# RMSNorm factors from one constant product over split sums of squares, in a two-layer decoder trunk

## The chip, the cores and the metric

The kernel runs on one core of one Trainium2 chip. The metric is the device time of one execution in microseconds, and lower is better. TensorE (PE) multiplies matrices, ScalarE (ACT) evaluates functions and copies, VectorE (DVE) does elementwise work, GpSimd (POOL) does little here, and SyncE (SP) issues nearly all DMAs. Each engine runs its own queue in order and waits on semaphores of the others. PE writes its results to PSUM, eight banks of 128 x 512 fp32; operands lie in SBUF, which has 128 partitions.

## The reference

The input is one sequence of 1024 tokens with 1024 channels. There are two layers. The first mixes tokens with a gated linear recurrence, the second with stick-breaking attention of 16 heads. Each is followed by a SwiGLU feed-forward network (FFN) of width 2816. An RMSNorm stands ahead of each of these four sub-layers and one more at the end.

```python
def rms_norm(x, g):
    xf = x.astype(jnp.float32)
    y = xf * lax.rsqrt(jnp.mean(xf * xf, axis=-1, keepdims=True) + RMS_EPS)
    return (y * g.astype(jnp.float32)).astype(x.dtype)

def reference(...):
    h = x
    for layer in range(2):
        hn = rms_norm(h, mix_norm[layer])
        mixed = rg_lru_block(hn, ...) if layer == 0 else stick_breaking_attention(hn, ...)
        h = h + mixed
        h = h + swiglu_ffn(rms_norm(h, ffn_norm[layer]), ffn_w_in[layer], ffn_w_out[layer])
    return rms_norm(h, final_norm)
```

All inputs and the output are fp32.

## The kernel before

**Layout.** Activations lie transposed: channels are on partitions, in 8 blocks of 128, and tokens run along the free axis, in two halves of 512 (`n` = 0, 1). One tile of 128 x 512 is one block of one half.

**Precision.** Every operand of a large product is split into a high and a low part of a shorter format (fp32r): a copy on ACT gives the high part, a subtraction on DVE gives the low part. A product is then three matmuls of 128x512, high x high, high x low and low x high (`mm3`, L598 to L600). The FFN also uses a scheme of seven products in place of eight (products 0, 1, 2, 3, 4, 6, 5 in this order, each of four `mm3`), so that combinations of weights and of activations are formed on DVE.

**The norm.** The gain is folded into the activations ahead of the product, and the factor 1/sqrt(mean + eps), one number for each token, is multiplied onto the product's result. So it is needed late, but it is needed on all 128 partitions. For each half the kernel gathers the squares of the 8 blocks in one 128 x 512 tile (`sacc`, `acc` or `rbc`) with ACT and DVE. What is left is a sum over the partitions, a root, and a copy to all partitions. That is done in four steps:

1. Sums: four fp32 matmuls with a 128x128 slice of the tile as the left operand and a column of ones as the right one. The sums come out as columns of 4 values, tokens on partitions (`column_stats`, `stats_mm`, `column_sums`).
2. Root: a small Sqrt on ACT and five or six small DVE instructions on 128x4 or 128x8, with one Newton step, to `rcol`.
3. Spread: four fp32 matmuls of 128x128 for each half. A column of `rcol`, read 128 times, is multiplied by the identity, which puts the factors along the free axis on all partitions (`spread`, L645; `factors`, L1381).
4. In the recurrence and in attention DVE copies the result to SBUF (`rbc`, L787 and L2178). The FFN reads it in PSUM (`ob`).

An fp32 matmul of this kind leaves two records in the profile, so four of them stand as x8.

**Order.** It is written out by hand for each engine. The four places are:

- *Recurrence.* PE multiplies the first four column groups for tokens of half 0, block by block as data arrive. Then it runs the four groups of half 1 (`second(0)` to `second(3)`, 24 matmuls each). Both halves' sums and spreads share the one bank that belongs to the fourth group. Behind this a planner (`lru_plan`) orders the rest from estimated costs.
- *FFN of each layer.* The first step (`f` = 0) is special; the norm stands in the loop's first pass (`s_ == 0`, `f` = 1): the sums behind the fourth product (`k == 3`) and the spreads behind the sixth (`k == 5`). DVE and ACT meanwhile split weights for this step and the next (`nw` is the next one: `a_lo` L1114, `s12`, `s2`, `s3` L1097 to L1103, `do_s4` L1106, `b_lo` L1123, `c_lo` L1133 and L1134), copy products out of PSUM (`post`, L1283 to L1296), and apply the gate (L1301 to L1307): the product of G and the factor, Silu, the factor again for the up branch, the product of the two. `b_lo` of a step stands behind the gate's first instruction of that step, and PE needs its result in the third matmul of the third product.
- *Attention.* `attention_plan` lists every task of the stage with an engine, an estimated cost and a rank. `Plan.emit` simulates the engines with these costs and emits the tasks in that order. A root of another table costs 1.3 there, and a handoff between engines 0.15. Queries and keys, multiplied by the factor, are split and moved by DMAs on SP's queue, and the first score product (`z`, L2035) needs them.

The final norm has a path of its own (`end_plan`, `finish`) and is not touched by the change.

## Time and profile before

| What | Value |
| --- | --- |
| time, median of 3 runs | 2174.35 us (2174.34 to 2174.76) |
| time of the profiled execution | 2175.16 us |
| span in the profile | 2173.0 us |
| PE busy | 2160.0 us, 99% of the span |
| DVE busy | 1709.4 us, 79% |
| ACT busy | 1086.4 us, 50% |
| granted PE clock | 1.0 over the whole span |

A row of the timeline has the start in us, the duration, the engine, the line of the kernel, the operation, output<-inputs by the program's names, shapes, and how many records are merged in it. In square brackets stands how long the engine idled ahead of it and who ended that wait. PEld rows are weight loads, which run beside PE's matmuls. The start of a matmul is recorded and its end is modelled: rows of PE overlap, so a cost on PE is read from one start to the next. The chain that ended last is followed back from the last instruction to whatever released each step.

### The profile page before, as it was taken

What the parts mean: (1) busy time and instruction counts of PE and PEld (TensorE: products, weight loads), DVE (VectorE), ACT (ScalarE), POOL (GpSimd) and SP (SyncE); (2) the same over time, 40 slices, a digit from 0 to 9 for tenths busy, and PEclk for the clock granted to TensorE, in tenths of its full rate; (3) what the DMA queues carried; (4) which work ended last, traced back from release to release, by engine and by line L of the source; (5) the groups of instructions that cost most, each with busy time, mean ns of one, the idle gap of its engine ahead of it and who ended that gap; (6) DMA issues with size and microseconds to landing.
All of it is one profiled execution on the core that took longest, in us unless ns stands there. A gap on an engine that the chain in (4) does not pass through costs nothing.

```text
span 2173.0 us, 27239 instructions
## 1 busy us (share of the span) xinstructions
PE 2160.0 (99%) x10066; PEld 1793.4 (83%) x10066; DVE 1709.4 (79%) x2429; ACT 1086.4 (50%) x1775; POOL 29.1 (1%) x38
## 2 busy tenths in 40 slices
PE   9999999999999999999999999999999999999998
PEld 7888888888888888888888888888888888888787
DVE  7988678667777887878888888877877777787887
ACT  5577445344444544555555555544534444454555
POOL 0000020000000000000000000002000000000000
PEclk9999999999999999999999999999999999999999
DMA  4111312344444753443333333542133444467442
GB/s 176 40 49 49 118 47 70 105 141 141 141 159 132 271 204 122 146 143 100 90 105 88 104 90 102 156 166 81 59 116 117 146 143 147 142 235 242 127 162 85
DMA packets 133317, 274.62 MB, mean 126 GB/s; under 512 B 15296, under 2 KB 23872, under 8 KB 133184
## 3 DMA queue, kind: packets, MB, share of 16 engines
q1 hardware_dynamic: 132768, 272.36, 38.5%
q8 instruction: 79, 1.29, 0.2%
q10 hardware_dynamic: 416, 0.52, 0.1%
q14 instruction: 54, 0.44, 0.1%
HBM read 176.88 MB, written 70.78 MB: 114 GB/s over the span
## 4 chain that ended last, share of the span: by engine, by line
PE 96%; DVE 2%; ACT 1%; issue 0%; DMA 0%; SPq 0%; POOL 0%; DVEq 0%; ACTq 0%; POOLq 0%
PE p_ps L600 18%; PE p_ps L598 18%; PE p_ps L599 18%; PE qk_ps L598 4%; PE qk_ps L600 4%; PE qk_ps L599 4%; PE z_ps L2035 3%; PE av_ps L2083 3%; PE wt_ps L2066 3%; PE a_ps L599 3%; PE a_ps L598 3%; PE a_ps L600 3%; PE ob_ps L599 2%; PE ob_ps L598 2%; PE ob_ps L600 2%; PE g_ps L599 1%
## 5 line engine op out<-in xcount | busy, mean ns | idle before, releaser
L598 PE MATMUL p_ps<-vh,wbh 128*128 128x512 f32 x524 | 204.4, 390 | 1.2 <-ACT ta L1741 1.2
L600 PE MATMUL p_ps<-vh,wal 128*128 128x512 f32 x524 | 204.4, 390 | 0.5 <-DVE wal L1114 0.4
L598 PE MATMUL p_ps<-vh,wch 128*128 128x512 f32 x524 | 204.5, 390 | 0.2 <-ACT held L1519 0.2
L600 PE MATMUL p_ps<-vh,wbl 128*128 128x512 f32 x524 | 204.5, 390 | 0.0
L600 PE MATMUL p_ps<-vh,wcl 128*128 128x512 f32 x524 | 204.3, 390 | 0.0
L599 PE MATMUL p_ps<-vl,wbh 128*128 128x512 f32 x524 | 204.1, 389 | 0.0
L598 PE MATMUL p_ps<-vh,wah 128*128 128x512 f32 x524 | 204.1, 389 | 0.0
L599 PE MATMUL p_ps<-vl,wch 128*128 128x512 f32 x524 | 204.1, 389 | 0.0
L599 PE MATMUL p_ps<-vl,wah 128*128 128x512 f32 x524 | 204.1, 389 | 0.0
L1119 ACT CAST wbh<-sb 128x1024 fp32r<-128x1024 f32 (+2 forms) x69 | 69.6, 1009 | 198.1 <-DVE sb L1103 198.1
L2047 ACT ACTIVATE F<-z_ps 128x512 f32<-128x512 f32 (+3 forms) x188 | 92.1, 490 | 99.3 <-PE z_ps L2035 97.9
L2071 ACT CAST th<-wt_ps 128x512 fp32r<-128x512 f32 x192 | 92.2, 481 | 84.3 <-PE wt_ps L2066 77.1
L2054 DVE TENSOR_TENSOR_SCAN F<-F,unit 128x128 f32<-128x128 f32 (+3 forms) x128 | 104.9, 821 | 33.4 <-ACT F L2047 32.4
L2075 DVE TENSOR_TENSOR tl<-wt_ps,th 128x512 fp32r<-128x512 f32 x192 | 104.7, 546 | 16.6 <-ACT th L2071 16.4
L600 PEld LDWEIGHTS p_ps<-vh,wal 128*128 128x128 f32 x524 | 98.4, 188 | 22.1 <-DVE wal L1114 1.8
L598 PEld LDWEIGHTS p_ps<-vh,wbh 128*128 128x128 f32 x524 | 98.4, 188 | 21.8 <-ACT ta L1741 1.6
L600 PEld LDWEIGHTS p_ps<-vh,wbl 128*128 128x128 f32 x524 | 98.4, 188 | 21.5 <-DVE wbl L1123 1.1
L598 PEld LDWEIGHTS p_ps<-vh,wch 128*128 128x128 f32 x524 | 98.4, 188 | 21.0 <-ACT held L1519 0.7
L600 PEld LDWEIGHTS p_ps<-vh,wcl 128*128 128x128 f32 x524 | 98.4, 188 | 20.8 <-DVE wcl L1133 0.3
L599 PEld LDWEIGHTS p_ps<-vl,wah 128*128 128x128 f32 x524 | 98.4, 188 | 20.5
L599 PEld LDWEIGHTS p_ps<-vl,wbh 128*128 128x128 f32 x524 | 98.4, 188 | 20.4
L599 PEld LDWEIGHTS p_ps<-vl,wch 128*128 128x128 f32 x524 | 98.4, 188 | 20.5
(430 smaller groups left out, 5499.1 us busy)
## 6 DMA issues: line engine op xcount, KB each, us to landing
raw<-in_ffn_w_in SPq DMA_DIRECT2D x88, 512.0 KB, 3.7
vl<-pd SPq DMA_DIRECT2D x128, 256.0 KB, 3.6
pd<-U SPq DMA_DIRECT2D x90, 256.0 KB, 2.3
raw<-in_ffn_w_out SPq DMA_DIRECT2D x28, 512.0 KB, 4.1
raw<-in_attn_w_qkv SPq DMA_DIRECT2D x24, 512.0 KB, 3.8
kh<-qh SPq DMA_DIRECT2D x64, 128.0 KB, 2.3
kl<-ql SPq DMA_DIRECT2D x64, 128.0 KB, 2.3
acc<-pd SPq DMA_DIRECT2D x28, 256.0 KB, 2.6
```

The costliest lines, as they stand in the source:

```text
L598: nc.tensor.matmul(ps, lhsT=wh, rhs=mh, start=first, stop=False, **kw)
L599: nc.tensor.matmul(ps, lhsT=wh, rhs=ml, start=False, stop=False, **kw)
L600: nc.tensor.matmul(ps, lhsT=wl, rhs=mh, start=False, stop=last, **kw)
L1119: nc.scalar.copy(self.full(self.wb), self.full(self.sb))
L2035: nc.tensor.matmul(ps[:, 0:n], lhsT=lhsT, rhs=rhs, start=i == 0, stop=i == 1)
L2047: nc.scalar.activation(F, Z.pop(c)[:, 0:n], AF.Sigmoid, scale=-SC)
L2054: V.tensor_tensor_scan(rev, rev, unit[:, NB - n :][:, ::-1], 0.0, op0=ALU.mult, op1=ALU.add)
L2066: nc.tensor.transpose(tp[:, c : c + P], F[:, (kb % 4) * P : (kb % 4 + 1) * P], ident)
L2071: nc.scalar.copy(WH[u][:, c:], TP[u][:, c:])
L2075: V.tensor_sub(WL[u][:, c:], TP.pop(u)[:, c:], f32(WH[u])[:, c:])
L2083: nc.tensor.matmul(ps[:, c:], lhsT=VV[q][:, kb, hx], rhs=t.pop(u)[:, c:], start=kb == 4 * G and i == 0, stop=kb == 3 and i == 1,)
```

## The change

At the four places the sums, the small root chain, the spread and the copy are replaced by a class `Factors`. For each half it does this:

- `hi`, `lo`: splits the tile of square sums into a high and a low part, one ACT copy and one DVE subtraction of 128x512;
- `sums`: two matmuls of 128x512. The left operand is one constant column (-2^-41, tile `minus`) read 128 times, so that every partition gets the sum for every token, in place;
- `root`: Abs_reciprocal_sqrt on ACT, 128x512 from PSUM, with scale and a bias operand that undo the constant;
- `square`: the square of that on ACT;
- `newton` and `out`: two DVE instructions of 128x512 which make one Newton step. In the FFN, `out` writes to PSUM, where the gate reads it.

In the recurrence both halves' sums stand between `second(0)` and `second(1)`, in the banks of the third and fourth column group. In the FFN, `hi` and `lo` stand at `k == 2`, the sums at `k == 4`, and the remaining four steps at `k == 4` too, behind `a_lo`, `s2` and `s3` of the next weights. They borrow one FFN tile and the two small tiles `ta` and `tb`. In attention the planner gets seven tasks for each half in place of five, with new costs. At the start there are two one-column memsets and one one-column copy more.

```diff
     for n in range(NH):
-        t = plan.add("pe", 0.95, fn["sums", n], [known["acc", n]], -17 + 2 * n)
-        t = plan.add("act", 0.25, fn["root", n], [t], -17 + 2 * n, "sqrt")
-        t = plan.add("dve", 1.0, fn["factor", n], [t], -17 + 2 * n)
-        t = plan.add("pe", 1.05, fn["spread", n], [t], -16 + 2 * n)
-        factors.append(plan.add("dve", 0.62, fn["rbc", n], [t], -16 + 2 * n))
+        t = plan.add("act", 0.5, fn["s_hi", n], [known["acc", n]], -17 + 2 * n)
+        t = plan.add("dve", 0.6, fn["s_lo", n], [t], -17 + 2 * n)
+        t = plan.add("pe", 0.46, fn["sums", n], [t], -17 + 2 * n)
+        t = plan.add("act", 0.62, fn["root", n], [t], -17 + 2 * n, "root")
+        t = plan.add("act", 0.5, fn["square", n], [t], -17 + 2 * n)
+        t = plan.add("dve", 0.66, fn["newton", n], [t], -17 + 2 * n)
+        factors.append(plan.add("dve", 0.66, fn["rbc", n], [t], -17 + 2 * n))
...
+    minus = cp.tile([P, 128], F32R, name="minus")
+    fresh = tiny[:, 60:61]
+    nc.gpsimd.memset(fresh, -(2.0**-41))
+    nc.vector.tensor_copy(minus[:, 0:1], fresh)
+    nc.gpsimd.memset(tiny[:, 61:62], EPS * 2.0**-20)
+
+    class Factors:
+        def __init__(self, src, hi, lo, ps, w, ww, out):
+            self.src, self.parts, self.ps, self.w, self.ww, self.to = src, (hi, lo), ps, w, ww, out
+        def hi(self):
+            nc.scalar.copy(self.parts[0], self.src)
+        def lo(self):
+            nc.vector.tensor_sub(self.parts[1], self.src, f32(self.parts[0]))
+        def sums(self):
+            for i, t in enumerate(self.parts):
+                nc.tensor.matmul(self.ps, lhsT=minus[:, 0:1].broadcast_to([P, P]), rhs=t, start=i == 0, stop=i == 1)
+        def root(self):
+            nc.scalar.activation(self.w, self.ps, AF.Abs_reciprocal_sqrt, bias=tiny[:, 61:62], scale=-(2.0**11))
+        def square(self):
+            nc.scalar.square(self.ww, self.w)
+        def newton(self):
+            nc.vector.scalar_tensor_tensor(self.ww, self.ps, -EPS * 2.0**-31, self.ww, op0=ALU.add, op1=ALU.mult)
+        def out(self):
+            nc.vector.scalar_tensor_tensor(self.to, self.ww, 1.5 * 2.0**-10, self.w, op0=ALU.add, op1=ALU.mult)
+        def rest(self):
+            self.root()
+            self.square()
+            self.newton()
+            self.out()
...
-        column_stats(sacc[0], bank, 0)
+        again = lambda k, dt=F32: sp.tile([P, NB], dt, tag=f"fr{k}", name="again")
+        sums = [
+            Factors(sacc[n], again(n, F32R), again(2 + n, F32R), pa[FIRST[3 - n]][1], rbc[n], again(4 + n), rbc[n])
+            for n in range(NH)
+        ]
+        sums[0].hi()
+        sums[0].lo()
         second(0, range(ND))
-        spread_to(0)
+        sums[1].hi()
+        sums[1].lo()
+        for t in sums:
+            t.sums()
+        for t in sums:
+            t.rest()
...
-        column_stats(sacc[1], bank, 1)
         second(1, range(ND))
-        spread_to(1)
         second(2, range(ND))
...
-            UT = [gp.tile([P, S], F32, name=f"U{i}") for i in range(3)]
+            GT, UT = [big("G", i) for i in range(2)], [big("U", i) for i in range(2)]
...
+            t = big("U", 2, F32R)
+            parts = (half(t, 0), half(t, 1)), [pair_tile(x, F32R) for x in ("ta", "tb")]
+            sums = [Factors(acc[n], *parts[n], half(ob, n), acc[n], rbc[n], half(ob, n)) for n in range(NH)]
...
-                        elif k == 3:
-                            stats_mm()
-                        elif k == 5:
-                            factors()
+                        elif k == 4:
+                            for t in sums:
+                                t.sums()
+                            UT.append(big("U", 2))
+                            ta, tb = (pair_tile(x) for x in ("ta", "tb"))
...
                         w.d_lo()
                         if nw:
                             nw.a_hi()
+                        if s_ == 0:
+                            for t in sums:
+                                t.hi()
+                                t.lo()
                     elif nw:
...
                             nw.a_lo()
                             nw.s2()
                             nw.s3()
+                            if s_ == 0:
+                                for t in sums:
+                                    t.rest()
...
+        def sums_hi(n):
+            SUM[n] = Factors(
+                rbc[n], own([P, NB], f"oo{n}", F32R, "oo"), own([P, NB], f"F{8 + n}", F32R),
+                bank(psO, "o", n, "st_ps"), own([P, NB], f"F{10 + n}"), own([P, NB], f"tl{n}"), rbc[n],
+            )
+            SUM[n].hi()
```

More of the change, by code (lines that the diff above doesn't have):

```diff
@@ L573, in trunk @@
     rcol = cp.tile([P, NT], F32, name="rcol")
-    cp.tile([P, 120], F32, name="edge_l")
+    minus = cp.tile([P, 128], F32R, name="minus")
[26 more added lines that the diff above has]
+            self.out()
     def load_raw(src):
@@ L628, in proc @@
             self.w[self.order[i]] = (k3(hi), k3(lo))
-    def rstd(dst, ms):
-        n = dst.shape[-1]
-        sq = cp.tile([P, max(n, 4)], F32, tag="rs_s", name="rs_s", bufs=2)[:, 0:n]
-        t = cp.tile([P, max(n, 4)], F32, tag="rs_t", name="rs_t", bufs=2)[:, 0:n]
-        nc.scalar.sqrt(sq, ms)
-        nc.vector.reciprocal(sq, sq)
-        nc.vector.tensor_mul(t, sq, sq)
-        nc.vector.tensor_mul(t, t, ms)
-        nc.vector.tensor_scalar(t, t, -0.5, 1.5, op0=ALU.mult, op1=ALU.add)
-        nc.vector.tensor_mul(dst, sq, t)
     def spread(ps, n, i0=0, i1=4):
@@ L651, in spread @@
             )
-    def broadcast_r(ps_pool, tag, n):
-        ps = ps_pool.tile([P, NB], F32, tag=tag, name="rb_ps")
-        spread(ps, n)
-        nc.vector.tensor_copy(rbc[n], ps)
-    def stats(acc, ps_pool, tag, n, i0=0, i1=4):
-        ps = ps_pool.tile([P, NB], F32, tag=tag, name="st_ps")
-        column_stats(acc, ps, n, i0, i1)
-    def column_stats(acc, ps, n, i0=0, i1=4):
-        for i in range(i0, i1):
-            nc.tensor.matmul(ps[:, i : i + 1], lhsT=acc[:, i * P : (i + 1) * P], rhs=ones, start=True, stop=True)
-        ms = cp.tile([P, 4], F32, tag="ms", name="ms", bufs=2)[:, i0:i1]
-        nc.vector.tensor_scalar(ms, ps[:, i0:i1], 1.0 / D, EPS, op0=ALU.mult, op1=ALU.add)
-        rstd(rcol[:, 4 * n + i0 : 4 * n + i1], ms)
     def squares(h, d, n, sqp, acc, eng=None, first=None):
@@ L725, in trunk @@
         sp = st.enter_context(tc.tile_pool(name="sp", bufs=1, reuse_waits="tile"))
-        one = lambda name, dt=F32: sp.tile([P, NB], dt, name=name)
+        one = lambda name, dt=F32: sp.tile([P, NB], dt, tag=name, name=name)
         fh = [one(f"fh{k}", F32R) for k in range(ND)]
@@ L783, in second @@
                 mm3(pa[FIRST[i]][1], fh[k][:, c], fl[k][:, c], xh[k][1], xl[k][1], k == 0, k == ND - 1)
-        def spread_to(n):
-            spread(bank, n)
-            nc.vector.tensor_copy(rbc[n], bank)
-        column_stats(sacc[0], bank, 0)
-        second(0, range(ND))
-        spread_to(0)
+        again = lambda k, dt=F32: sp.tile([P, NB], dt, tag=f"fr{k}", name="again")
[5 more added lines that the diff above has]
+        sums[0].lo()
+        second(0, range(ND))
+        sums[1].hi()
[4 more added lines that the diff above has]
+            t.rest()
         sm = lambda name: lc.tile([P, ND], F32, name=name)
@@ L1048, in mix_out_ffn_in @@
         sp_ = vs.enter_context(tc.tile_pool(name="sums", bufs=1, side="right", reuse_waits="tile"))
-        ta, tb = (sp_.tile([P, NB], F32, name=x) for x in ("ta", "tb"))
+        pair_tile = lambda x, dt=F32: sp_.tile([P, NB], dt, tag=x, name=x)
+        ta, tb = (pair_tile(x) for x in ("ta", "tb"))
         v = {}
@@ L1251, in mix_out_ffn_in @@
             gp = gs.enter_context(tc.tile_pool(name="gu", bufs=1, reuse_waits="tile"))
-            GT = [gp.tile([P, S], F32, name=f"G{i}") for i in range(2)]
-            UT = [gp.tile([P, S], F32, name=f"U{i}") for i in range(3)]
+            big = lambda x, i, dt=F32: gp.tile([P, S], dt, tag=f"{x}{i}", name=f"{x}{i}")
+            GT, UT = [big("G", i) for i in range(2)], [big("U", i) for i in range(2)]
             pd = [[dp.tile([P, NB], F32, name=f"pd{layer}_{p}_{i}") for i in range(8)] for p in range(NF // 2)]
@@ L1361, in mix_out_ffn_in @@
             nw.ready = True
-            def stats_mm():
-                st_ps = half(ob, 1)
-                for n in range(NH):
-                    for i in range(4):
-                        nc.tensor.matmul(
-                            st_ps[:, 4 * n + i : 4 * n + i + 1],
-                            lhsT=acc[n][:, i * P : (i + 1) * P],
-                            rhs=ones,
-                            start=True,
-                            stop=True,
-                        )
-                ms = cp.tile([P, NT], F32, tag="ms8", name="ms8", bufs=1)
-                V.tensor_scalar(ms, st_ps[:, 0:NT], 1.0 / D, EPS, op0=ALU.mult, op1=ALU.add)
-                rstd(rcol, ms)
-            def factors():
-                for b in range(NT):
-                    nc.tensor.matmul(
-                        ob[:, b * P : (b + 1) * P],
-                        lhsT=rcol[:, b : b + 1].broadcast_to([P, P]),
-                        rhs=ident,
-                        start=True,
-                        stop=True,
-                    )
+            t = big("U", 2, F32R)
+            parts = (half(t, 0), half(t, 1)), [pair_tile(x, F32R) for x in ("ta", "tb")]
+            sums = [Factors(acc[n], *parts[n], half(ob, n), acc[n], rbc[n], half(ob, n)) for n in range(NH)]
             VISITS = (
@@ L1798, in mix_out_ffn_in @@
                                 squares(h, *sq_todo.pop(0), rbc, acc, V)
-                        elif k == 3:
-                            stats_mm()
-                        elif k == 5:
-                            factors()
+                        elif k == 4:
+                            for t in sums:
+                                t.sums()
+                            UT.append(big("U", 2))
+                            ta, tb = (pair_tile(x) for x in ("ta", "tb"))
                     if k == 0:
@@ L2148, in trunk @@
         }
-        def column_sums(n):
-            ST[n] = ps = bank(psO, "o", n, "st_ps")
-            for i in range(4):
-                nc.tensor.matmul(ps[:, i : i + 1], lhsT=rbc[n][:, i * P : (i + 1) * P], rhs=ones, start=True, stop=True)
-        small = [[tiny[:, 8 * i + 4 * n : 8 * i + 4 * n + 4] for i in range(3)] for n in range(NH)]
-        def root(n):
-            nc.scalar.activation(small[n][0], ST[n][:, 0:4], AF.Sqrt, bias=tiny[:, 63:64], scale=1.0 / D)
-        def factor(n):
-            q, m, t = small[n]
-            V.tensor_scalar(m, ST[n][:, 0:4], 1.0 / D, EPS, op0=ALU.mult, op1=ALU.add)
-            V.reciprocal(q, q)
-            V.scalar_tensor_tensor(t, m, -0.5, q, op0=ALU.mult, op1=ALU.mult)
-            V.tensor_mul(t, t, q)
-            V.scalar_tensor_tensor(rcol[:, 4 * n : 4 * n + 4], t, 1.5, q, op0=ALU.add, op1=ALU.mult)
-        def spread_out(n):
-            ST[n] = ps = bank(psO, "o", n, "rb_ps")
-            spread(ps, n)
-        ST = {}
-        acts |= {
-            "sums": column_sums,
-            "root": root,
-            "factor": factor,
-            "spread": spread_out,
-            "rbc": lambda n: V.tensor_copy(rbc[n], ST[n]),
+        SUM = {}
+        def sums_hi(n):
[4 more added lines that the diff above has]
+            SUM[n].hi()
+        acts |= {
+            "s_hi": sums_hi,
+            "s_lo": lambda n: SUM[n].lo(),
+            "sums": lambda n: SUM[n].sums(),
+            "root": lambda n: SUM[n].root(),
+            "square": lambda n: SUM[n].square(),
+            "newton": lambda n: SUM[n].newton(),
+            "rbc": lambda n: SUM[n].out(),
         }
```

## The prediction

> **What bounds the kernel now.** First I read the page for the share of each engine and the chain that ended last:

> ```profile
> span 2173.0 us, 27239 instructions
> PE 2160.0 (99%) x10066; PEld 1793.4 (83%) x10066; DVE 1709.4 (79%) x2429; ACT 1086.4 (50%) x1775; POOL 29.1 (1%) x38
> ...
> PE 96%; DVE 2%; ACT 1%; issue 0%; DMA 0%; SPq 0%; POOL 0%; DVEq 0%; ACTq 0%; POOLq 0%
> ```

> TensorE (PE) is busy for 2160.0 of 2173.0 us and makes 96% of the chain. So time goes only if PE gets less to do, and it comes back wherever PE then waits for VectorE (DVE), which is 79% busy. An average can't say where that is, so next comes the timeline of each of the four places.

> The profiled execution took 2175.16 us, 0.81 above the median of 2174.35; the sum is made against it and the answer is given against the median. I take 0.2% (4.35 us) as about what a measurement of this kernel can tell from no change.

> **Place 1, the recurrent layer.** PE's timeline there, with DVE's rows between:

> ```profile
> 28.60 0.39 PE L600 MATMUL a_ps<-xh,fl 128*128 128x512 f32 x1
> ...
> 29.00 3.87 DVE L756 TENSOR_TENSOR sacc<-sacc,sq 128x512 f32<-128x512 f32 x5
> ...
> 29.95 0.40 PE L599 MATMUL a_ps<-xl,fh 128*128 128x512 f32 x1
> ...
> 35.06 0.40 PE L600 MATMUL a_ps<-xh,fl 128*128 128x512 f32 x1
> ...
> 37.14 1.05 PE L664 MATMUL a_ps<-ones,sacc 128*128 128x1 f32 x8 [0.78 <-DVE rbc L787]
> ...
> 38.37 0.40 PE L599 MATMUL a_ps<-xl,fh 128*128 128x512 f32 x1
> ...
> 43.48 0.40 PE L600 MATMUL a_ps<-xh,fl 128*128 128x512 f32 x1
> ...
> 44.84 0.39 PE L599 MATMUL a_ps<-xl,fh 128*128 128x512 f32 x1
> ```

> From 29.95 to 35.06 lie 22 steps of a 128x512 matmul, so one costs 0.232 us. Each norm group is the distance between the rows that enclose it, less two such steps: 1.35 - 0.46 = 0.89, then 3.31 - 0.46 = 2.85 (a spread, PE's 0.78 wait for the copy that empties the shared bank, and a sum), then 1.36 - 0.46 = 0.90. That is 4.64 us. The new code puts four 128x512 products there, 4 x 0.232 = 0.93. Their left operand is one column read 128 times, as that of the spreads (`rcol`) already is, so 0.232 stands for it; were each to cost two such steps, 0.93 more, which I take as the upper bound. Nothing points below 0.232.

> Cover: the last square sum is there at 32.87 (29.00 + 3.87). The high part on ScalarE (ACT) and the low part on DVE follow, about 0.62 + 0.69 and two handoffs, at 34.3; PE, without its first group, arrives at 28.60 + 25 x 0.232 = 34.4 and needs that low part last of four, at 35.1. No wait; with the cover gone up to 0.3 us. The sums use the banks of the third and fourth column group, which PE overwrites after one more group, at about 40.9. The chain root, square, Newton, product for both halves (a table load of 1.28 included) ends near 39. DVE can then start on the columns near 40, where now the last spread is made only after 43.48; that is no less than PE gains, so nothing new is late behind it. The memsets and the one-column copy fall before 4.41, where DVE waits for its first data:

> ```profile
> 4.41 0.43 DVE L762 CAST fh<-fr 128x512 fp32r<-128x512 f32 x1 [4.41 <-DMA fr<-in_lru_first]
> ...
> 4.76 0.72 ACT L744 ACTIVATE xh<-xr,vc 128x512 fp32r<-128x512 f32 x1
> ...
> 5.39 0.61 ACT L752 ACTIVATE sacc<-xr 128x512 f32<-128x512 f32 x1
> ```

> Place 1: -4.64 + 0.93 = **-3.7** (to -2.5).

> **Places 2 and 4, the second step of each FFN.** PE, ACT and DVE in the first FFN, and two DVE rows of attention for a price:

> ```profile
> 346.99 0.39 PE L600 MATMUL p_ps<-vh,wcl 128*128 128x512 f32 x1
> ...
> 347.41 0.59 ACT L1289 COPY U<-p_ps 128x512 f32<-128x512 f32 x1 [0.66 <-PE p_ps L600]
> 348.02 1.28 ACT L635 ACT_TABLE_LOAD   x1
> ...
> 349.09 0.17 DVE L1376 TENSOR_SCALAR ms<-ob 128x8 f32<-128x8 f32 x1 [2.19 <-PE ob L1368]
> 349.24 0.40 PE L599 MATMUL p_ps<-vl,wbh 128*128 128x512 f32 x1
> ...
> 349.31 0.21 ACT L635 ACTIVATE rs_s<-ms 128x8 f32<-128x8 f32 x1
> ...
> 351.98 0.59 ACT L1291 COPY U<-p_ps 128x512 f32<-128x512 f32 x1 [2.46 <-PE p_ps L600]
> ...
> 352.60 0.69 DVE L1292 TENSOR_TENSOR U<-U 128x512 f32<-128x512 f32 x1 [1.43 <-ACT U L1291]
> ...
> 354.27 0.39 PE L600 MATMUL p_ps<-vh,wd 128*128 128x512 f32 x1
> ...
> 354.95 0.68 DVE L1103 TENSOR_TENSOR sb<-raw 128x512 f32<-128x512 f32 x1
> 355.55 0.68 DVE L1294 TENSOR_TENSOR G<-G,p_ps 128x512 f32<-128x512 f32 x1
> ...
> 356.52 0.39 PE L599 MATMUL p_ps<-vl,wch 128*128 128x512 f32 x1
> ...
> 363.38 1.22 DVE L1123 TENSOR_TENSOR wbl<-sb,wbh 128x1024 fp32r<-128x1024 f32 x1
> ...
> 364.71 0.19 PEld L600 LDWEIGHTS p_ps<-vh,wbl 128*128 128x128 f32 x1
> 364.93 0.39 PE L600 MATMUL p_ps<-vh,wbl 128*128 128x512 f32 x1
> ...
> 966.16 0.68 DVE L2178 COPY rbc<-rb_ps 128x512 f32<-128x512 f32 x1
> ...
> 966.88 0.69 DVE L1972 TENSOR_TENSOR t<-qk_ps,rbc 128x512 f32<-128x512 f32 x1
> ```

> Again by enclosing rows: 22 steps from 349.24 to 354.27 give 0.229 a matmul. The sums cost 2.25 - 0.46 = 1.79, the spreads the same, together 3.59. Four products cost 0.91. By PE's work alone: 3.59 - 0.91 = 2.67 less.

> But look at the rows from 363.38. DVE finishes the low part of the next weights (L1123) at 364.60, and PE loads them at 364.71. PE has 0.11 us to spare there, and DVE has been at it from 352.60 without a pause but for one wait for the Silu, which stays. So PE can only gain if that DVE chain ends earlier. In program order:

> - The four split instructions (two copies on ACT, two subtractions on DVE) stand after the third product, where the old kernel's DVE waits 2.19 us for PE's sums; two subtractions of 0.69 fit in, and PE needs them only after one more product. The small root chain (L1376 on) goes; it stood in DVE's next wait, 1.43 before L1292, so its going frees nothing.
> - The DVE chain starts when ACT has copied product 4. That product no longer has the sums ahead of it, so the chain starts 1.79 earlier: 352.60 becomes 350.81, and the point before L1294, 355.55, becomes 353.76.
> - Right there stand four new DVE instructions: Newton and final product for two halves. A 128x512 DVE instruction is 0.69 long; the next starts after 0.60 if independent (L1103 to L1294), and after 0.72 if it needs the result (L2178 to L1972, the last two rows). Two of each: 2.64 us. So L1294 begins at 356.40, 0.85 later than before.
> - ACT is not late for them: copy at 350.19, table load to 352.06, root 0.72 (L744's form, with a pointer) to 352.79, square 0.62 to 353.41; DVE arrives at 353.76. The second half has about 0.4 to spare.

> All that follows in DVE moves by 0.85: L1123 ends at 365.45. PE, which would load those weights at 364.71 - 2.67 = 362.04, waits until 365.50. The load thus moves by 0.79 and its matmul, if it starts with the load, by 0.57 at least: **+0.7 per FFN**. The 2.67 saved are lost, and a little more. Bounds: four instructions 0.60 apart give +0.4, 0.72 apart +0.95. No row shows DVE writing PSUM, which the final product does here; I price it as a read of PSUM, 0.68 (L1294). The second FFN has the same rows 1206.4 us later and the same margin:

> ```profile
> 1569.80 1.21 DVE L1123 TENSOR_TENSOR wbl<-sb,wbh 128x1024 fp32r<-128x1024 f32 x1
> ...
> 1571.12 0.19 PEld L600 LDWEIGHTS p_ps<-vh,wbl 128*128 128x128 f32 x1
> ```

> The load row shows 1.28 us, beginning 0.02 after the copy before it and followed at once by the root. [...]

> **Place 3, attention.**

> ```profile
> 960.24 0.40 PE L600 MATMUL qk_ps<-vh,wlo 128*128 128x512 f32 x1
> ...
> 961.61 0.40 PE L599 MATMUL qk_ps<-vl,whi 128*128 128x512 f32 x1
> ...
> 963.88 0.40 PE L600 MATMUL qk_ps<-xg,wlo 128*128 128x512 f32 x1
> ...
> 966.14 0.39 PE L599 MATMUL qk_ps<-xg,whi 128*128 128x512 f32 x1
> ...
> 967.05 0.39 PE L600 MATMUL qk_ps<-vh,wlo 128*128 128x512 f32 x1
> ...
> 968.40 0.39 PE L599 MATMUL qk_ps<-vl,whi 128*128 128x512 f32 x1
> ```

> By enclosing rows, with 0.227 a step: 0.92 + 1.81 + 0.90 = 3.62 (rounded), and four products cost 0.91: -2.7. In PE's waits the one that follows from this is:

> ```profile
> PE z_ps L2035 <- DMA kl<-ql: 1.0, 1, 1.0
> ```

> That is the first score product, which needs norm factors, split, and SP's DMAs of q and k. Whether PE arrives there 2.7 earlier and waits as much longer depends on the planner, which fixes the order from its own costs. Its old chain from sum to factor is 0.95 + 0.25 + 1.0 + 1.05 + 0.62, a table switch of 1.3 and four handoffs of 0.15: 5.8. The new one is 0.5 + 0.6 + 0.46 + 0.62 + 0.5 + 0.66 + 0.66 + 1.3 + 0.6: 5.9. So it still expects the score at the same time, while PE is free 2.7 earlier; it should put further V projections ahead of the score. The change issues no DMA; SP's queue only moves with the factors. I take -2.7. Bounds: -3.7 if the wait goes, 0 if PE arrives early and waits; the reordered rest adds or takes about 1.

> **Sum.** -3.7 + 0.7 + 0.7 - 2.7 = -5.0: 2175.16 becomes 2170.2, the median 2174.35 becomes **2169.3**. With the bounds the forecast's own range is -3.7 + 0.8 - 3.7 = -6.6 to -2.5 + 1.9 + 0 = -0.6: 2167.8 to 2173.8.

> **Rivals.**

> - *The whole PE saving arrives* (0.13). The FFN chain on DVE is shorter than I think, so PE keeps 2.67 twice: -3.7 - 5.3 - 2.7 = -11.7, 2162.6. For it: PE is 99% busy. Against it: the margin of 0.11.
> - *Attention gives nothing* (0.20). PE comes early to the score and waits for the DMAs: -3.7 + 1.4 = -2.3, 2172.0, no measurable change. For it: PE already waits 1.0 there. Against it: the planner's equal chains.
> - *Slower: root and square don't share a table* (0.11). Then each place has three more loads of 1.28 between root, square, root, square. In an FFN the second square ends near 358.5, and DVE comes to L1294 at 359.9 instead of 356.4: +0.7 becomes +4.2. In place 1 PE waits about 1.5 for the bank, and attention's factor comes 3.8 later, using up its gain. -2.2 + 8.4 + 0.5 = +6.7, 2181. It decides when the second square comes over 0.4 us late. For it: the code orders the four calls alternately. Against it: the old kernel's squares run between functions of several tables without a load of their own. [...]
> [...]

> **How the numbers follow.** My forecast has 0.53; by its own bounds 0.42 of that lies below 2170.0 and 0.11 within 0.2%. With the rivals: faster 0.42 + 0.13 = 0.55; same 0.11 + 0.17 + 0.03 = 0.31; slower 0.03 (from the second rival, if the order then also loses) + 0.11 = 0.14. The range 2162.0 to 2173.8 takes in the first rival and the forecast's own bounds and leaves out the third rival and some of the attention reorder.

> **What would show it.** In each FFN, a PE wait of about 3.3 us at L600 for `wbl` of L1123, which the old kernel has not. In place 1 no wait for `rbc`, and PE's third column group some 3.7 earlier. In attention the wait for `kl` near 1 us. One table load per root pair. I am wrong if the FFN wait is missing or far from 3.3, if loads stand before squares, or if the end of attention waits differently.

## The result, and the profile after

The changed kernel takes 2199.04 us (2198.66 to 2200.22) against 2174.34 us, a ratio of 1.0115, 95% interval 1.0100 to 1.0129: 1.1% slower, where 2169.3 us and a gain of 0.2% had been forecast, and outside the range of 2162.0 to 2173.8.

The head of the page of the changed kernel, then its chain of work:

```profile
span 2196.7 us, 27021 instructions
PE 2178.4 (99%) x9954; PEld 1784.1 (81%) x9954; DVE 1716.7 (78%) x2416; ACT 1098.2 (50%) x1793; POOL 29.1 (1%) x40
...
PE 97%; DVE 2%; ACT 1%; issue 0%; DMA 0%; SPq 0%; DVEq 0%; ACTq 0%
```

PE has 112 records fewer than before (9954 for 10066), and yet it is busy 18.4 us longer (2178.4 for 2160.0). So most of the loss isn't waiting. The waits of PE, longest first, in us in total, times, longest:

```profile
PE p_ps L640 <- ACT G L1304: 5.1, 2, 2.5
PE p_ps L642 <- DVE wbl L1144: 2.3, 2, 1.2
```

Both are new, one pair in each FFN, 3.7 us a pair (L640 and L642 are the high x high and low x high lines of `mm3`, L598 and L600 before). The wait for `rbc` is gone, as foreseen. The wait for `kl`, which was expected to stay near 1 us, is no longer in the list either. The groups of the page show where the busy time went (busy us, mean ns of one). First a row of the kernel before, then the same product after, which has nothing to do with the norm:

```profile
L598 PE MATMUL p_ps<-vh,wch 128*128 128x512 f32 x524 | 204.5, 390 | 0.2 <-ACT held L1519 0.2
```

```profile
L640 PE MATMUL p_ps<-vh,wch 128*128 128x512 f32 x524 | 207.6, 396 | 0.0
```

The large matmuls whose weights come from the two weight pools have become a little longer: 390 to 396 ns here, 389 to 394 for `a_ps` and `ob_ps` of `xh` and `whi`, 390 to 395 for `o_ps` of `vh` and `we`, hardly (434 to 435) for `qk_ps` of `vh` and `whi`. One product of 12 matmuls in the steady loop of the first FFN, from its first matmul to the first of the next product, before and after (the fence of after holds three such products, of `wch`, `wbh` and `wd`):

```profile
440.64 0.39 PE L598 MATMUL p_ps<-vh,wbh 128*128 128x512 f32 x1
...
443.36 0.39 PE L598 MATMUL p_ps<-vh,wch 128*128 128x512 f32 x1
```

```profile
447.86 0.40 PE L640 MATMUL p_ps<-vh,wch 128*128 128x512 f32 x1
...
450.63 0.40 PE L640 MATMUL p_ps<-vh,wbh 128*128 128x512 f32 x1
...
453.40 0.39 PE L640 MATMUL p_ps<-vh,wd 128*128 128x512 f32 x1
...
456.15 0.40 PE L640 MATMUL p_ps<-vh,wch 128*128 128x512 f32 x1
```

2.72 us became 2.77, and 2.75 for the product with `wd`. No engine is waited for in between, and the granted clock is 1.00 there. What differs is where the tiles lie: those of the weights, which PE loads (9954 records of PEld for 9954 of PE), and those of the moving operands, the activations. The change takes one further line out, which nobody uses, and with it the small tiles of the old chain:

```diff
-    cp.tile([P, 120], F32, name="edge_l")
...
+    minus = cp.tile([P, 128], F32R, name="minus")
```

The pool `cp` is the first on the left side of SBUF. It loses 480 bytes a partition with `edge_l` and 224 with the tiles `ms`, `rs_s`, `rs_t` and `ms8`, and gains 512 with `minus`. So every large tile that is stacked from the left (the moving operands `xh` and `xl`, a part of the FFN's moving operands `vh` and `vl`, the FFN's `G` and `U`, q and k) lies 192 bytes lower. The weights of the two pools, the residual stream and the rest of `vh` and `vl`, stacked from the right, lie where they did. Before, those weights and `xh`, `xl`, `vh` and `vl` all began at an address that leaves a remainder of 128 when divided by 256. One pair of the kernel before did not match: the recurrence's first weights, `fh` and `fl`, lie on the left with remainder 0.

### The profile page after: what moved, and what is told of

Its sections match the earlier page's. It is cut to its first block, busy times and chain, and to the rows that moved or that the text cites. A ratio compares the mean times of both kernels' runs of the same rounds, so it can differ in the third digit from the quotient of the medians.

```text
span 2196.7 us, 27021 instructions
## 1 busy us (share of the span) xinstructions
PE 2178.4 (99%) x9954; PEld 1784.1 (81%) x9954; DVE 1716.7 (78%) x2416; ACT 1098.2 (50%) x1793; POOL 29.1 (1%) x40
## 3 DMA queue, kind: packets, MB, share of 16 engines
q8 instruction: 78, 1.28, 0.2%
## 4 chain that ended last, share of the span: by engine, by line
PE 97%; DVE 2%; ACT 1%; issue 0%; DMA 0%; SPq 0%; DVEq 0%; ACTq 0%
PE p_ps L640 19%; PE p_ps L642 19%; PE p_ps L641 19%; PE qk_ps L640 4%; PE qk_ps L642 4%; PE qk_ps L641 4%; PE z_ps L2042 3%; PE av_ps L2090 3%; PE wt_ps L2073 3%; PE a_ps L640 3%; PE a_ps L642 3%; PE a_ps L641 3%; PE ob_ps L640 2%; PE ob_ps L642 2%; PE ob_ps L641 2%; PE g_ps L640 1%
## 5 line engine op out<-in xcount | busy, mean ns | idle before, releaser
L640 PE MATMUL p_ps<-vh,wbh 128*128 128x512 f32 x524 | 209.9, 400 | 6.3 <-ACT G L1304 5.1
L642 PE MATMUL p_ps<-vh,wbl 128*128 128x512 f32 x524 | 208.6, 398 | 2.3 <-DVE wbl L1144 2.3
L640 PE MATMUL p_ps<-vh,wah 128*128 128x512 f32 x524 | 207.6, 396 | 0.0
L640 PE MATMUL p_ps<-vh,wch 128*128 128x512 f32 x524 | 207.6, 396 | 0.0
L642 PE MATMUL p_ps<-vh,wal 128*128 128x512 f32 x524 | 206.7, 395 | 0.0
L642 PE MATMUL p_ps<-vh,wcl 128*128 128x512 f32 x524 | 206.3, 394 | 0.0
L640 PEld LDWEIGHTS p_ps<-vh,wbh 128*128 128x128 f32 x524 | 99.3, 190 | 28.4 <-ACT G L1304 6.0
L642 PEld LDWEIGHTS p_ps<-vh,wbl 128*128 128x128 f32 x524 | 99.4, 190 | 28.2 <-DVE wbl L1144 4.0
L642 PEld LDWEIGHTS p_ps<-vh,wal 128*128 128x128 f32 x524 | 98.3, 188 | 25.1 <-DVE wal L1135 1.2
L642 PEld LDWEIGHTS p_ps<-vh,wcl 128*128 128x128 f32 x524 | 98.4, 188 | 24.0 <-DVE wcl L1154 0.2
L640 PEld LDWEIGHTS p_ps<-vh,wch 128*128 128x128 f32 x524 | 98.6, 188 | 21.3
```

What stands on the lines that cost most here:

```text
L640: nc.tensor.matmul(ps, lhsT=wh, rhs=mh, start=first, stop=False, **kw)
L642: nc.tensor.matmul(ps, lhsT=wl, rhs=mh, start=False, stop=last, **kw)
```

## The experiments

Each is compared with the kernel before on the same chip, whose median was 2173.63, 2174.18 and 2173.66 us in the three groups of runs. Theory A: the place of the left side's tiles makes the matmuls slower. Theory B: the new instructions and waits do it.

**1. The changed kernel with the old places.**

```diff
     minus = cp.tile([P, 128], F32R, name="minus")
+    cp.tile([P, 48], F32, name="edge_l")
```

> The changed kernel with 192 bytes of padding behind the constant tile, so that every tile that follows lies at the address it has in the kernel before. Theory A (the changed kernel's matmuls are slower because its left-hand SBUF tiles moved by 192 bytes): the step of a 128x512 matmul in the FFN returns from 0.231 to 0.227 us, and what is left is -3.7 in the recurrence, -3 in attention, and in each FFN -2.67 of PE work + 3.65 of waiting + about 2.3 of reduced clock, together about 0: 2174 us. Theory B (the slower step comes from the new instructions themselves or from the waits): nothing changes, 2199 us and 0.231.

Measured: 2175.15 us, ratio 1.0008 (0.9999 to 1.0017). PE's row:

```profile
PE 2152.6 (99%) x9954; PEld 1783.2 (82%) x9954; DVE 1716.2 (79%) x2416; ACT 1099.4 (51%) x1793; POOL 29.2 (1%) x40
```

192 bytes of unused space take 25.8 us off PE's busy time (2178.4 to 2152.6) with the same 9954 records. A product takes 2.72 us again. Theory B is refuted for the large part; the new instructions and waits leave the kernel about where it was before.

**2. and 3. The kernel before with the left side moved**, by 192 bytes (`edge_l` 72 words) and by 128 (88 words), and no instruction changed.

```diff
-    cp.tile([P, 120], F32, name="edge_l")
+    cp.tile([P, 72], F32, name="edge_l")
```

> The kernel before with its padding tile cut from 120 to 72 words, so that the left-hand tiles lie 192 bytes lower, as in the changed kernel; no instruction changes. Theory A: the FFN step rises to 0.231, the recurrence's triple of matmuls from 0.680 to 0.687, and the time to about 2174 + 22 = 2196 us. Theory B: 2174 us, 0.227.

> The kernel before with the padding tile cut from 120 to 88 words: the left-hand tiles lie 128 bytes lower. Theory A in a strict form (any move away from the right-hand tiles' residue costs): slower, some 2185 to 2196 us. Theory A with a grid of 128 bytes: 2174 us as before, since every left-hand tile still lies on a multiple of 128. Theory B: 2174 us.

Measured: 2198.03 us, ratio 1.0113 (1.0099 to 1.0127), and 2201.0 us, 1.0127 (1.0113 to 1.0141). PE's rows, for 192 and for 128 bytes:

```profile
PE 2184.3 (99%) x10066; PEld 1793.4 (82%) x10066; DVE 1708.9 (78%) x2429; ACT 1086.4 (49%) x1775; POOL 29.0 (1%) x38
```

```profile
PE 2186.5 (99%) x10066; PEld 1793.7 (82%) x10066; DVE 1707.0 (78%) x2429; ACT 1086.1 (49%) x1775; POOL 29.2 (1%) x38
```

The move alone gives the old kernel the loss of the changed one. The shift by 128 bytes costs no less, and more than the 2185 to 2196 us expected for it, so a grid of 128 bytes is out. The starts of the same matmuls in the four timelines, taken apart by stage (us more than before; the stages end at the first matmul of `ob_ps`, `p_ps`, `qk_ps`, `p_ps` and `o_ps` and at the last matmul):

| stage | after | change at the old places | before, left side moved |
| --- | --- | --- | --- |
| recurrence to `ob_ps`, with place 1 | -2.2 | -3.8 | +2.0 |
| rest of the recurrence | +0.9 | 0.0 | +0.9 |
| first FFN | +14.3 | +3.7 | +10.3 |
| attention | -2.4 | -3.7 | +1.1 |
| second FFN | +12.8 | +4.1 | +9.0 |
| output | +0.2 | 0.0 | +0.2 |
| sum | +23.6 | +0.3 | +23.4 |

The two causes add up, in the sum (0.3 + 23.4) and in each stage to 0.4 us.

**4. The old norm in the FFNs**, the new one in the recurrence and in attention, all tiles at the places of before. In `ffn` the old `stats_mm` and `factors` are put back:

```diff
-                        elif k == 4:
-                            for t in sums:
-                                t.sums()
...
+                        elif k == 3:
+                            stats_mm()
+                        elif k == 5:
+                            factors()
```

> New factors in the recurrence and in attention only, the old column sums, root chain and spreads in both FFNs, and padding so that all tiles lie as in the kernel before. Theory A: no wait in the FFNs, -3.7 and -3.0 remain: 2167.6 us. Theory B (the new instructions bring the slow step from the recurrence on): 2185 us or more.

Measured: 2167.03 us, ratio 0.9969 (0.9958 to 0.9981): 6.6 us faster than before. PE's wait at the first score:

```profile
PE z_ps L2068 <- DMA kl<-ql: 0.4, 1, 0.4
```

The two places that gain are the recurrence and attention; the new norm costs 2175.15 - 2167.03 = 8.1 us in the two FFNs. `kl` is waited for 0.4 us where it was 1.0 (0.3 in experiment 1), so PE does not come there earlier in vain.

**5. and 6. What the FFN's loss is made of.** The timeline of experiment 1 in the first FFN (in brackets the idle time ahead of the row and what ended it):

```profile
346.98 1.28 ACT L601 ACT_TABLE_LOAD   x1
...
348.27 0.69 ACT L601 ACTIVATE acc<-ob,tiny 128x512 f32<-128x512 f32 x1
...
350.66 0.70 DVE L610 SCALAR_TENSOR_TENSOR ob<-rbc,acc 128x512 f32<-128x512 f32 x1
...
351.40 0.69 ACT L601 ACTIVATE acc<-ob,tiny 128x512 f32<-128x512 f32 x1 [1.77 <-DVE ob L610]
...
352.79 0.69 DVE L607 SCALAR_TENSOR_TENSOR rbc<-ob,rbc 128x512 f32<-128x512 f32 x1 [1.42 <-ACT rbc L604]
...
354.12 0.68 DVE L1316 TENSOR_TENSOR G<-G,p_ps 128x512 f32<-128x512 f32 x1
...
358.93 1.22 DVE L1329 TENSOR_TENSOR U<-U,G 128x1024 f32<-128x1024 f32 x1
...
360.24 0.59 ACT L1305 COPY G<-p_ps 128x512 f32<-128x512 f32 x1 [1.10 <-DVE U L1329]
...
361.93 1.21 DVE L1145 TENSOR_TENSOR wbl<-sb,wbh 128x1024 fp32r<-128x1024 f32 x1
```

```profile
360.88 0.50 PE L641 MATMUL p_ps<-vh,wbh 128*128 128x512 f32 x1 [2.72 <-ACT G L1305]
...
363.20 0.80 PE L643 MATMUL p_ps<-vh,wbl 128*128 128x512 f32 x1 [1.58 <-DVE wbl L1145]
363.79 0.63 PE L641 MATMUL p_ps<-vh,wbh 128*128 128x512 f32 x1
364.22 0.63 PE L642 MATMUL p_ps<-vl,wbh 128*128 128x512 f32 x1
...
367.16 0.40 PE L641 MATMUL p_ps<-vh,wch 128*128 128x512 f32 x1
```

The root of the second half (ACT, 351.40) stands idle for 1.77 us until DVE has written the first half's factor to `ob` (L610). Both halves are parts of the one PSUM tile `ob`; the second root reads its own half and yet waits for the write to the other. Experiment 5 takes that order away. DVE then waits 1.42 us for the second square. The whole DVE chain is late by that, up to the gate (L1329), which frees `G` for the next copy, and to `wbl` (L1145). PE waits twice, 4.30 us together. Behind that it steps by 0.43 us a matmul, not 0.227, for a few matmuls. The windows show a lower clock there (the length of the window, the busy us of PE, PEld, DVE, ACT and POOL, each with its number of instructions, then the granted PE clock, the DMA share and GB/s):

```profile
360.00:362.00 2.00, 0.73 (x2) 0.30 (x2) 1.97 (x4) 0.59 (x1) 0.00 (x0) 1.00 0.48 178
362.00:364.00 2.00, 0.80 (x2) 0.71 (x3) 2.00 (x4) 1.06 (x1) 0.00 (x0) 0.79 0.24 88
364.00:366.00 2.00, 2.00 (x6) 1.52 (x6) 2.00 (x3) 0.00 (x0) 0.00 (x0) 0.50 0.35 45
366.00:368.00 2.00, 2.00 (x9) 1.64 (x8) 0.07 (x1) 0.64 (x2) 0.00 (x0) 0.86 0.54 217
```

Experiment 5 takes the calls in another order, both roots first; experiment 6 loads the root's table earlier and puts `b_lo` (which makes `wbl`) ahead of the gate as well. All three are at the places of before.

```diff
-                                    t.rest()
+                                    t.root()
+                                for t in sums:
+                                    t.square()
+                                for t in sums:
+                                    t.newton()
+                                for t in sums:
+                                    t.out()
```

```diff
+                        elif k == 3:
+                            nc.scalar.activation(tiny[:, 59:60], tiny[:, 61:62], AF.Abs_reciprocal_sqrt)
...
+                if s_ == 1 and not w.ready:
+                    w.b_lo()
                 if gf is not None and s_:
                     gate(gf, 0)
                 if not w.ready:
-                    w.b_lo()
+                    if s_ != 1:
+                        w.b_lo()
```

> The padded changed kernel (2175.15 us) with one more edit in the feed-forward stages: the two root reads come first, then the two squares, then the two Newton factors, then the two output products, so that the second root no longer waits 1.42 us and more for the first output product, which shares the tile `ob` with it. Theory (the 3.7 us net loss per feed-forward stage is a late chain of root, square, Newton, product and `b_hi`, plus a few matmuls at half clock after the long wait): the PE waits for `G` and `wbl` shrink by about 1.4 us together and the slow matmuls behind them become fewer, so 2170 to 2172.5 us; if the low clock goes away altogether with the shorter wait, about 2168. Rival (the waits are set by the reading of `GT` by the gate and by the table load, not by the second root): 2174.5 to 2175.5, no change.

> As the kernel with the reordered factors, with two more edits: a one-element Abs_reciprocal_sqrt is issued earlier in the stage, so that the table is loaded before the sums end, and `b_lo` of the first weight pair is issued ahead of the gate of the last hidden tile. Theory: the second wait (`wbl`) goes below 1 us and the first one (`G`, held by the gate that reads `GT`) becomes the only one, so 2165 to 2170 us, below the version with the old path in the feed-forward stages (2167.03) if the clock stays up. Rival (moving `b_lo` ahead only delays the gate and with it the `G` copy by the same 0.6 us): no better than the reordered kernel, within 0.7 us of it.

Measured: 2171.33 us, ratio 0.9987 (0.9978 to 0.9997), and 2167.06 us, ratio 0.9968 (0.9956 to 0.9980). PE's waits, for experiment 5 and then for experiment 6:

```profile
PE p_ps L643 <- DVE wbl L1145: 3.2, 2, 1.6
PE p_ps L641 <- ACT G L1305: 2.7, 2, 1.4
```

```profile
PE p_ps L641 <- ACT G L1305: 2.4, 2, 1.2
...
PE p_ps L643 <- DVE wbl L1145: 0.9, 2, 0.5
```

In experiment 5 the wait for `G` fell from 2.7 to 1.4 us a stage, 1.3 of the 1.4 expected. So the second root's wait made that half of it; the other 1.4 and the wait for `wbl`, which stayed at 1.6, have other causes. In experiment 6 L1316 starts here:

```profile
349.77 1.28 DVE L607 SCALAR_TENSOR_TENSOR rbc<-ob,rbc 128x512 f32<-128x512 f32 x2
...
351.09 1.44 DVE L610 SCALAR_TENSOR_TENSOR ob<-rbc,acc 128x512 f32<-128x512 f32 x2
352.44 0.68 DVE L1316 TENSOR_TENSOR G<-G,p_ps 128x512 f32<-128x512 f32 x1
```

352.44 is 1.7 earlier than in experiment 1. The FFN stages now take 0.6 and 0.0 us less than before. Experiments 4 and 6 both beat the kernel before by 0.3% and can't be told from one another; experiment 6 had been expected to come out below experiment 4 if the clock stays up.

**7. Experiment 5 with the early table load alone**, without the earlier `b_lo` (the first two added lines above).

> The kernel with the reordered factors (2171.33 us) and the early one-element Abs_reciprocal_sqrt, without the earlier `b_lo`. If the table load in front of the first root is what the rest of the gain of the kernel with both edits rests on: 2167 to 2168.5 us, the waits for `G` 1.2 us and for `wbl` below 1 us in each stage. If the earlier `b_lo` gave it, which alone takes the second wait from 1.6 to 0.5 us and so keeps the total below what lowers the clock: 2170.5 to 2171.5 us, with half clock behind the waits as before.

Measured: 2171.11 us, ratio 0.9986 (0.9977 to 0.9995), the same as experiment 5. So the earlier `b_lo`, on top of the early load, gave the gain of experiment 6: with it, the wait for `wbl` goes from 1.6 to 0.5 us, and it is the second half of each stall. The expectation of half clock behind the waits in both stages held in one of them only. Windows of experiment 7, in the first FFN:

```profile
362.00:364.00 2.00, 2.00 (x11) 1.65 (x10) 2.00 (x4) 0.00 (x0) 0.00 (x0) 1.00 0.22 18
364.00:366.00 2.00, 2.00 (x11) 1.65 (x10) 1.17 (x3) 1.89 (x3) 0.00 (x0) 1.00 0.61 244
...
1564.00:1566.00 2.00, 1.30 (x3) 1.12 (x4) 2.00 (x4) 0.60 (x1) 0.00 (x0) 0.69 0.00 0
1566.00:1568.00 2.00, 2.00 (x6) 1.54 (x6) 1.58 (x2) 0.00 (x0) 0.00 (x0) 0.50 0.47 119
```

The last two rows are of the second FFN. Both have waits of 1.2 and 1.58 us; 11 matmuls in 2 us follow in the first, 6 in the second. Of the ten runs three took 2169.1 to 2169.3 us, the profiled one among them, and seven 2170.9 to 2171.8. That would fit a clock lowered in one FFN or in both, but only the one run has a profile.

**8. and 9. Is it the address or the distance?** Experiment 8 moves the left side of the kernel before by 256 bytes (`edge_l` 56 words). Experiment 9 moves both sides by 192 bytes:

```diff
-    edge.tile([P, 24], F32, name="edge")
+    edge.tile([P, 72], F32, name="edge")
...
-    cp.tile([P, 120], F32, name="edge_l")
+    cp.tile([P, 72], F32, name="edge_l")
```

> The kernel before with `edge_l` cut from 120 to 56 words and nothing else: every tile of the left side 256 bytes lower, with the same remainder of its address by 256. If the remainder decides what a matmul costs (128 at left and right gives 2.720 us for the 12 matmuls of a product): 2174 us, ratio 1.000. If it is the distance between the two sides, or any move from the present place that costs: 2190 to 2201.

> The kernel before with `edge_l` cut from 120 to 72 words and `edge` at the right end raised from 24 to 72 words: every tile of both sides, weights too, 192 bytes lower, with the difference between any two of them as before. If the address itself decides (remainder 128 by 256 is the quick one): slow, at least the 2198.03 us of the kernel in which the left side alone was moved, and more evenly 2.77 us for every product of 12 matmuls, since now every operand has moved. If what counts is that left and right operands match: 2174 us.

Measured: 2174.27 us, ratio 1.0000 (0.9990 to 1.0009), and 2174.72 us, ratio 1.0002 (0.9993 to 1.0012). PE's row of experiment 9:

```profile
PE 2159.3 (99%) x10066; PEld 1792.5 (82%) x10066; DVE 1709.2 (79%) x2429; ACT 1086.4 (50%) x1775; POOL 29.1 (1%) x38
```

The address itself didn't matter here: moved together by 192 bytes, both sides were as quick as before (PE busy 2159.3 us for 2160.0). What counted was the place of one side against the other: a distance changed by 256 bytes cost nothing (2174.27 us), while changes of 128 and 192 cost 1.3 and 1.1% (2201.0 and 2198.03 us).

**10. The weights against the rest.** As experiment 2, with 48 words left free behind the weight pools on the right side, so that everything but the weights lies 192 bytes lower.

```diff
             self.two = self.stk.enter_context(tc.tile_pool(name="wq", bufs=2, side="right", reuse_waits="tile"))
+            gap = self.stk.enter_context(tc.tile_pool(name="gap", bufs=1, side="right"))
+            gap.tile([P, 48], F32, name="gap")
```

> The kernel before with `edge_l` cut from 120 to 72 words and 48 words left free on the right side behind the weight pools: all tiles but the weights lie 192 bytes lower, on both sides alike; the weights stay. Theory (a matmul is slowed by the place of its moving operand against the place of the weights loaded beside it; a change of place from one moving operand to the next adds to it): every product of 12 feed-forward matmuls takes what the one product with all its moving operands shifted took in the kernel with only the left side moved, 2.746 us against 2.720, so about half of the loss there (2198 less 2174): 2183 to 2193 us. Rival (only moving operands among one another count, the weights do not): 2.720 us a product and 2174 us.

Measured: 2189.73 us, ratio 1.0074 (1.0057 to 1.0090), within the 2183 to 2193 expected. PE's row, and products with `wch` and with `wd`:

```profile
PE 2174.8 (99%) x10066; PEld 1793.1 (82%) x10066; DVE 1708.7 (78%) x2429; ACT 1086.4 (50%) x1775; POOL 29.2 (1%) x38
```

```profile
446.48 0.39 PE L600 MATMUL p_ps<-vh,wch 128*128 128x512 f32 x1
...
449.23 0.39 PE L600 MATMUL p_ps<-vh,wbh 128*128 128x512 f32 x1
...
451.97 0.39 PE L600 MATMUL p_ps<-vh,wd 128*128 128x512 f32 x1
...
454.72 0.39 PE L600 MATMUL p_ps<-vh,wch 128*128 128x512 f32 x1
```

All products take 2.75 us now, with `wd` and without. In the changed kernel `wd` is the product whose moving operands all lie on the moved side, and it took 2.75 as well. So a shift of all moving operands by 192 bytes against the weights cost 0.03 us a product (1%, 2.72 to 2.75), and a mixture of moved and unmoved ones, as the other products of the changed kernel have, another 0.02 (2.77). That a mixture is the dearer is no rule: at 128 bytes (experiment 3) `wd` took 2.80 us and the mixed products 2.76 to 2.78. What in a mixture costs was not taken apart.

## Why the prediction was wrong, step by step

- **The sum, "-3.7 + 0.7 + 0.7 - 2.7 = -5.0": it lacked a term.** Every term was a distance between matmuls near the four places. None was for the thousands of matmuls that the change does not touch, and none could be, since the place of the tiles wasn't looked at. "So time goes only if PE gets less to do, and it comes back wherever PE then waits" took the price of those matmuls as fixed; it went from 2.72 to 2.77 us for twelve. The missing term is about +24 us (2198.03 - 2173.63 = 24.4 in experiment 2, 2199.04 - 2175.15 = 23.9 from experiment 1 to the changed kernel). This decided the sign. A hint stood in the prediction's own rows: 0.232 us a step in place 1, where `fh` and `fl` don't match their moving operands, against 0.229 and 0.227 in the other places.
- **"Place 1: -3.7": right.** -3.8 at the old places (experiment 1). The four products of 128x512 follow without a wait, at the price of 0.23 each that was taken from the rows; in the changed kernel:

```profile
33.94 0.39 PE L642 MATMUL a_ps<-xh,fl 128*128 128x512 f32 x1
34.17 1.08 PE L597 MATMUL a_ps<-again,minus 128*128 128x512 f32 x4
35.09 0.40 PE L640 MATMUL a_ps<-xh,fh 128*128 128x512 f32 x1
```

- **"+0.7 per FFN": the mechanism was right, the size wrong.** PE's saving of 2.67 is lost to a late DVE chain and a new wait, as written. Measured is +3.7 and +4.1. Two terms were missed, 1.4 for the second root's wait and, behind the stall, 1.7 (first FFN) and 2.6 (second) at the low clock. In the first FFN they make up the difference: 0.7 + 1.4 + 1.7 = 3.8. In the second they give 4.7, 0.6 more than measured, which stays open; that stage of the kernel before itself took 617.1 us in its profile and 615.9 in experiment 8.
  - "ACT is not late for them ... The second half has about 0.4 to spare" failed: the second root waits for the first half's output on `ob`, and DVE 1.42 us for the second square. L1294 was put at 356.40, which is 352.6 with place 1's 3.8 taken off; L1316, the same instruction, starts at 354.12 in experiment 1 and, without that wait and with an early table load, at 352.44 in experiment 6. So the four DVE instructions themselves were priced right.
  - Behind the stall PE's granted clock was 0.50 (364 to 366 in experiment 1): from 363.20 to 367.16 there are 10 steps, 3.96 us where 2.27 would do, 1.7 lost. In the second FFN, with 0.51 from 1570 to 1575, there are 13 steps from 1569.57 to 1575.11, 5.54 us for 2.95.
- **"A PE wait of about 3.3 us ... for `wbl`": partly.** It shows as two waits, 2.72 for `G` and then 1.58 for `wbl`. The copy to `G` is held by the gate of the last hidden tile on the same late DVE chain, ahead of `wbl`. The prediction followed the chain to `wbl`, where it does end, and passed over that copy.
- **"Attention: -2.7": right, with more.** -3.7 at the old places, the bound for the case that the wait for `kl` goes. The wait was expected to stay near 1 us and fell to 0.3 (experiment 1), which would be 0.7 of the 1.0 more; the rest was not followed up. PE does not wait at the first score in place of the work removed.
- **The rivals.** "Root and square don't share a table", the one on the slower side, is out: four table loads of 1.28 us at the root's line, one a place, and none ahead of a square. "The whole PE saving arrives" did not happen in any run: even experiment 6 keeps at most 0.6 of the 2.67. The kernel became slower by none of them. No run shows what the last term in the chance of "same", 0.03, needs, a table load that costs more than its row: in experiment 1 the load of 1.28 us starts at 346.98 and the root at 348.27, 0.01 behind its end.

So the forecast of the change's own work, -5.0, stands against +0.3 in the profiles (the table's middle column; +1.5 by the medians, 2175.15 against 2173.63): it misses by 3.0 and 3.4 us in the two FFNs, with 1.0 given back by attention and 0.1 by place 1. The other 24 us came with the places of the tiles, from lines that compute nothing.

## What to carry to other kernels

In this kernel, whose PE is 99% busy, the time of a matmul was a common factor: twelve of them took 2.77 us for 2.72, and the kernel about 24 us more. Before costing a change by its own instructions, ask whether it moves the tiles, weights against moving operands: a constant added, a scratch tile dropped or a tag shared shifts everything that is stacked behind it. Where a tile looks unused, such as `edge_l`, try it before removing it, and when every matmul of a trace is longer by 1 or 2%, compare the addresses first. And where two halves share one tile, write the steps of a chain for both halves side by side (root, root, square, square), not one half after the other: here a write to one half held up a read of the other by 1.77 us.

## What the runs showed of the hardware

```profile
59.82 0.39 PE L598 MATMUL a_ps<-xh,whi 128*128 128x512 f32 x1
...
65.40 0.40 PE L598 MATMUL a_ps<-xh,whi 128*128 128x512 f32 x1
```

`fh` and `fl` are off `xh` and `xl` by a remainder of 128 in all twelve kernels, and in every one a step with them took 0.232, in the kernel before too. That this is a little of the same loss is an estimate, from 0.232 against 0.227; no run has them matched.

Against experiment 9, experiment 10 changed only the place of the weights, and PE was busy 15.5 us longer (2174.8 for 2159.3). Which part of the hardware makes it so is not settled, nor whether a distance of remainder 0 by 256 is the only quick one; moves by 0, 128, 192 and 256 bytes were tried.

**PE's clock behind a stall.** The windows show 1.00 ahead of and well behind a stall and 0.50 in a slow stretch; values between (0.79 and 0.86 in experiment 1, 0.69 in experiment 7) stand in windows at the edge of one. Behind waits of 4.3 us in two parts (experiment 1) it was 0.50 in the first FFN (364 to 366) and 0.51 in the second (1570 to 1575). Behind waits of 2.78 us (experiment 7) it was 0.50 in the second FFN (1566 to 1568) and 1.00 in the first (362 to 366). In experiment 6 waits of 1.66 us in two parts lowered it in the second FFN and not in the first:

```profile
362.00:364.00 2.00, 2.00 (x11) 1.65 (x10) 2.00 (x4) 1.57 (x4) 0.00 (x0) 1.00 0.25 18
...
1564.00:1566.00 2.00, 2.00 (x6) 1.58 (x5) 2.00 (x4) 0.66 (x1) 0.00 (x0) 0.50 0.07 16
```

So it wasn't the length of the wait alone that decided here. Two matmuls lie between the two waits (1561.30 and 1561.63 in the second FFN), and once the clock fell behind 1.66 us of waiting; what decided was not shown. Where the clock fell, the stall cost 1.5 to 2.6 us more than its own length: 1.5 and 1.6 in experiment 5, 1.7 and 2.6 in the two FFNs of experiment 1, and 2.1 in the first FFN of the changed kernel itself (10 steps from 365.89 to 370.31, 4.42 us for 2.3).
